# Hybrid pooling/SSD layer on one core: the scan's tables in one stretch, rounded sums, a weight split behind the mixer's last square, first loads on two queues, clearing later

## The chip, the cores and the metric

One Trainium2 chip, one core. The time is device microseconds of a whole execution of the kernel, the median of three executions. One execution of the kernel before was also taken by the profiler; views of that profile and its trace are what is read below. Engines are called by their names in the profile: PE is TensorE (its matmuls; PEld its weight loads), DVE VectorE, ACT ScalarE, POOL GpSimd, SP SyncE, which here issues most DMAs. "SPq" and "ACTq" rows are the DMA issues of those engines.

## The reference

One layer of a streaming encoder, for 256 frames of a new stream and 32 next frames of a running one. Both share all weights, so the kernel treats them as 288 columns. D_MODEL is 2048, the scan has 32 heads of 64 with a state of 128, and the feed-forward width is 5632. Cut to its core:

```python
xn   = rmsnorm(x, norm_mix_pre)
proj = xn @ w_in                                  # [u 1024 | z 2048 | xBC 2560 | dt 32]
y_pool = pool_mixer(u, ...)                       # trailing means over 2, 4, 8, 16 frames, times w_pool
xbc = silu(causal_dwconv(xbc)); dt = softplus(dt_raw + dt_bias)
acum = cumsum(dt * -exp(a_log)) in chunks of 64
y = chunked scan of xs, dt, B, C, acum, D         # decays exp(acum_i - acum_j) and exp(acum_last - acum)
y_ssd = rmsnorm per group (y * silu(z))
x  = x + rmsnorm(concat[y_pool, y_ssd] @ w_out, norm_mix_post)
hn = rmsnorm(x, norm_ffn_pre)
x  = x + rmsnorm((silu(gate) * val of causal_dwconv(hn @ w_up)) @ w_down, norm_ffn_post)
```

The outputs are the new x of both streams and all their new histories and states.

## The kernel before, in words

**Layout and the three products.** Features lie on the 128 partitions and the 288 frames along the columns. Every weight product in float32 is made of three rounded ones (`mm3`, L140 to L143): weight and activation are each split into a high half (rounded to fp32r) and a low half (the rest, rounded), and high x high, high x low and low x high are added in PSUM. The high half of a weight is a copy on ACT (L135), the low half a subtraction on DVE (L136), both in `split_w` in pieces of 1024 columns (512 where the piece is that narrow). `project` (L145 to L173) runs a group of output tiles over the depth of the weight: it fetches a piece (`fetch_w`, L116, issued by SP), splits it and issues its matmuls. Its arguments `wait`, `hold` and `behind` put the splits or the matmuls behind named instructions.

**Order.** A scheduler places the instructions on each engine by priorities and by its own model of the time. What is written `pin(...)` (`keep_in_program_order`) keeps the order of the program on its engine; `issue_after` puts an instruction behind another; `high_priority` draws it forward. Each engine takes its list in order.

**Start.** The input's first tile and the first weights are loaded in chunks (`CHUNKS`, L44: six of one row of 128, then five of two), each 768 columns wide, that is, six output tiles: four of B and C and two of the pool's input. SP issues all of these loads one after the other, but for the first third of chunk 0, which ACT issues (`first_load`, L207; `input_load`, L201; order L215 to L227). Chunk 0 is loaded and split in three column pieces (`PIECES`, L205), chunk 1 is loaded whole and split in three pieces, later chunks in one (`prepare`, L269 to L308: the input's halves at L281 and L284, the weight's at L293 and L297; for chunk 0 the first high third is made by DVE at L304, the others by ACT at L302, the lows by DVE at L307). `BUSY` (L45) matmuls on a constant tile (L264) run ahead of the first real ones. In chunk 0 the 18 matmuls go by half first and column block second (L344). GpSimd clears eight padded buffers for the convolutions (`ebuf`, `ubuf`, L330 to L332); they are first needed behind the last chunk. Squares of the input (L314, L317) are added up along the way; their sum over the partitions is one float32 matmul with ones, `prs` (L348), in the middle of the last chunk but one, and gives the root-mean-square factor `rstd` (L351, L352). The 32 columns of dt follow in float32 (L361).

**Scan's tables.** While TensorE goes on with the x part of the input projection, dt, its running sums `g` (32 heads on partitions, 416 columns in three blocks) and the decays `dec` are made on DVE and ACT (L471 to L510). They are turned so that frames lie on partitions: for each of three blocks, three transposes of 32 x 128 (`g`, `dt`, `dec`) into a PSUM tile of its own (L517 to L519) and two copies out. Then `pwq` (L526: three small matmuls that copy the last 32 rows of the turned decays to three places), `phv` (L535, L536: per-head factors spread over partitions), and `pcb`, the products of B and C, once for each of two groups (L552 to L554), masked into `cbt` (L555 to L558). Each of these stands where the scheduler puts it between the weight matmuls. Behind them come eight quads of heads (`ssd_quad`, L585), whose DVE and ACT work builds decay matrices and whose 16 float32 matmuls `py` each (L616 to L622) stand between weight matmuls. `sel`, `pick` and `sel64` (L376 to L378) are small constant tables for `phv`.

**Sums of the gated groups.** `rstd_all` (L662) sums squares over partitions by one float32 matmul with ones and takes the root and its reciprocal: `rg0` (L752) and `rg1` (L774) for the two groups of the scan, `r2` (L1086) for the feed-forward.

**Mixer's end.** The last output tile of w_out goes through `mix_out` (L842). The sum of the squares of all tiles but the last, `msum`, is rounded on ACT (L863) and its low half made on DVE (L864); the last tile is squared on ACT (L860), rounded on DVE (L861), its low half made on DVE (L864). Four rounded matmuls add the four parts over partitions (`psum_m`, L869), among the matmuls of the scan's final state (L950, L951). Then the root on ACT (`rm`, L1002) and its reciprocal on DVE (L1003), and for each of 16 tiles the scaling, the residual and the split of `hn` (L1014 to L1024), on which the first matmuls of the up projection wait. That projection's first call (`up`, L1077; L1100) has four groups of weights: three of 256 columns and one of 128, each in depths of four, so the last group's piece is 512 wide. All pieces of its first depth may be split before `hn` is there; later depths are held behind the first `hn` (`hold`).

Of the kernel before, what the change touches and what calls it, by code (L numbers as in the profile page):

```python
# [44 lines left out]
BUSY = 14  # L45
# [11 lines left out]
def body(  # L57
# [87 lines left out]
    def project(view, groups, acts, ksplit, before=None, done=None, spare=(), hold=(), behind=None, wait=()):  # L145
# [7 lines left out]
        for i, (kb, n) in enumerate(ksplit):  # L153
# [5 lines left out]
            for raw, (c0, w) in zip(raws, groups):  # L159
                parts = split_w(raw, kb, n, w, tuple(wait) + ((after or ()) if m0 else ()) + (hold if i else ()))  # L160
# [40 lines left out]
    def input_load(k0, k1):  # L201
        c = slice(KD + NT * k0 if k0 else 0, KD + NT * k1)
        pin(sp.dma_start(out=xg[:, c], in_=x_g[:, c]))
# [3 lines left out]
    def first_load(i):  # L207

        kb, n = CHUNKS[i]
        raw = wpool.tile([P, n, NB], F32, tag="raw" if n > 1 else ("hi", "lo")[i % 2], name="raw")  # L210
        for j, c in enumerate((slice(0, NB),) if i else PIECES):
            pin((sp if i or j else act).dma_start(out=raw[:, :, c], in_=w_first[:, kb : kb + n, c]))
        raws.append(raw)
# [3 lines left out]
    for i, (k0, k1) in enumerate(zip(INPUT[:-1], INPUT[1:])):  # L217
        input_load(k0, k1)
# [50 lines left out]
    def prepare(i):  # L269
# [19 lines left out]
        if i:  # L289
            for t in tiles:  # L290
                high(t)
            for c in PIECES if i == 1 else (slice(0, NB),):
                pin(act.activation(hi[:, :, c], raw[:, :, c], AF.Copy))  # L293
            for t in tiles:
                low(t)
            for c in PIECES if i == 1 else (slice(0, NB),):
# [26 lines left out]
    for i, (kb, n) in enumerate(CHUNKS):  # L323
# [4 lines left out]
        if i == 5:  # L328
            first_load(10)
            with tc.issue_after(lows[-1].ins):  # L330
                for e in ebuf + ubuf:
                    pin(pool.memset(e, 0.0))  # L332
# [4 lines left out]
        if i == len(CHUNKS) - 2:  # L337
            pin(dve.tensor_tensor(sq2[:, :NT], sq2[:, :NT], sq2[:, NT:], op=ALU.add))
        w = ahead_w.pop(0)
# [3 lines left out]
        if i == 0:  # L343
            products.sort(key=lambda q: (q[0], q[3]))  # L344
        for q, (r, m, k, x) in enumerate(products):
            if i == len(CHUNKS) - 2 and q == 24:
                p_ = aux([P, NT], "prs")
                pin(pe.matmul(p_, ones, sq2[:, :NT], start=True, stop=True))  # L348
# [23 lines left out]
    sel = const.tile([HEADS, 2], F32, name="sel")  # L372
    pick = const.tile([HEADS, NX], F32, name="pick")
    sel64 = const.tile([HEADS, 2, 64], F32, name="sel64")
    with tc.issue_after(last_split[1].ins):
        dve.tensor_reduce(sel, id32.rearrange("h (t r) -> h r t", r=2), axis=AX.X, op=ALU.add)  # L376
        dve.tensor_reduce(pick, id32.rearrange("h (t r) -> h t r", r=2), axis=AX.X, op=ALU.add)
        dve.tensor_copy(sel64, sel.unsqueeze(2).broadcast_to([HEADS, 2, 64]))  # L378

# [4 lines left out]
    mp = mixer.enter_context(tc.tile_pool(name="mixer", bufs=1))  # L384
    sc_stage = const.tile([P, 2, 3, NXC], F32, name="sc_stage")
# [109 lines left out]
    g = mp.tile([HEADS, 4, MW], F32, tag="m", bufs=2, name="g")[:, 0, :]  # L495
# [11 lines left out]
    dec = htile("dec", tag="gsum")  # L507
    for (o, n), go, last in zip(BLK, (0, 256, 384), (255, 383, 415)):
        act.activation(dec[:, o : o + n], g[:, go : go + n], AF.Exp, bias=g[:, last : last + 1], scale=-1.0)
    dve.tensor_tensor(dec, dec, dt, op=ALU.mult)  # L510


    tok = mp.tile([P, 3, 2, HEADS], F32, name="tok")
    tokd = const.tile([P, 3, HEADS], F32, name="tokd")
    for b, (o, go) in enumerate(((0, 0), (P, 256), (TAIL, MW - P))):
        p_ = aux([P, 3, HEADS], "ptok")
        pe.transpose(p_[:, 0, :], g[:, go : go + P], id32)  # L517
        pe.transpose(p_[:, 1, :], dt[:, o : o + P], id32)
        pe.transpose(p_[:, 2, :], dec[:, o : o + P], id32)  # L519
        dve.tensor_copy(tok[:, b, :, :], p_[:, 0:2, :])  # L520
        dve.tensor_copy(tokd[:, b, :], p_[:, 2, :])

    p_ = aux([P, HEADS], "pwq")
    wq = const.tile([P, HEADS], F32, name="wq")
    for j in range(3):
        pe.matmul(p_[NS * j : NS * (j + 1), :], ident[:, P - NS :], tokd[:, 2, :], start=True, stop=True)  # L526
    dve.tensor_copy(wq[: 3 * NS], p_[: 3 * NS])
# [6 lines left out]
    p_ = aux([P, NX + HEADS], "phv")  # L534
    pe.matmul(p_[:, :NX], sel64.rearrange("h r q -> h (r q)"), hv[:, :NX], start=True, stop=True)  # L535
    pe.matmul(p_[:, NX:], ones[:HEADS, :], hv[:, NX:], start=True, stop=True)  # L536
# [12 lines left out]
    for gi in range(2):  # L549
        blocks_out(b_d, gi, bc[gi], mp, 2)  # L550
        p_ = aux([P, MW], "pcb")
        pe.matmul(p_[:, 0:256], bc[gi][:, 0:P], bc[2 + gi][:, 0:NP_], start=True, stop=True)  # L552
        pe.matmul(p_[:, 256:384], bc[gi][:, P:NP_], bc[2 + gi][:, P:NP_], start=True, stop=True)
        pe.matmul(p_[:, 384:], bc[gi][:, TAIL:], bc[2 + gi][:, NP_:], start=True, stop=True)  # L554
# [107 lines left out]
    def rstd_all(sq, scale, name, pin=False):  # L662

        p_ = aux([P, NT], "psum_t")
        ins = pe.matmul(p_, ones, sq, start=True, stop=True)
        if pin:
            tc.keep_in_program_order(ins)
            sums_at.append(ins)
        with tc.high_priority(offset=800 if pin else 0):
# [73 lines left out]
    for i in range(NX // 2):  # L743
# [7 lines left out]
        if i == 5:  # L751
            rg.append(rstd_all(gsum[0], 0.25 / 1024, "rg0"))  # L752
# [21 lines left out]
    rg.append(rstd_all(gsum[1], 0.25 / 1024, "rg1"))  # L774
# [62 lines left out]
    ones_r = op_.tile([P, P], F32R, name="ones_r")  # L837
    act.activation(ones_r, ones, AF.Copy)
# [3 lines left out]
    def mix_out(p_):  # L842
# [9 lines left out]
        else:  # L852
            with tc.high_priority(offset=400):
# [3 lines left out]
                for i, q in enumerate((msum, last_sq)):  # L857
                    h_ = op_.tile([P, NT], F32R, tag="sq", bufs=2, name="mhi")
                    if i:
                        pin(act.activation(q, p_, AF.Square))  # L860
# [3 lines left out]
                    pin(dve.tensor_tensor(parts[i], q, h_.bitcast(F32), op=ALU.subtract))  # L864
                    parts.append(h_)

# [500 lines left out]
```

## Time and profile before

| | |
|---|---|
| median of three executions | 1331.42 us (1331.05 to 1332.49) |
| the profiled execution | 1331.79 us |
| its span in the profile | 1330.1 us |
| instructions | 25269 |
| DMA traffic | 251.74 MB, mean 189 GB/s |
| input projection's start (first chunk to the dt columns) | 5.69 to 48.4 us of the span |
| scan's tables | about 100 to 117 us |
| mixer's end | 472 to 479 us |

The span runs from the first to the last recorded instruction; the execution's own time holds 1.7 us more. In the views, times are microseconds from the span's start. A row of the timeline gives start and busy time, engine, line and operation, what it writes and reads with the shapes, and, in brackets, how long the engine had been idle before it and what ended that. "x4" is a run of four such instructions shown as one row. The chain of waits follows the work that ended last back from the end: its rows give the start, the time that the piece adds and the engine, tile and line. The busy time of a matmul in the timeline overlaps with its neighbours'; the step from one start to the next is what it costs. A table by stretches gives each engine's busy share (instructions in brackets), the granted clock of TensorE, the busy share of the DMA engines and GB/s.

### The profile page before, as it was taken

To read this page: it belongs to the slowest core of one execution; us is meant where nothing else is said; L and a number is where in the kernel's file an instruction comes from. 1 tells how busy PE (TensorE), PEld (TensorE's weight loads), DVE (VectorE), ACT (ScalarE), POOL (GpSimd) and SP (SyncE) were. 2 spreads that over 40 slices of the span, in tenths; PEclk is the share of its full clock that TensorE was granted. 3 is DMA by queue.
4 is the path that set the end of the run, shared out by engine and by line. 5 is a ranking of instruction groups with operands and counts; after the bars stand their busy time and mean duration, and the time that the engine had idled before them with its cause. 6 is when DMAs were issued, how large, how long until landed. Compare 5 with 4: busy or idle time off the path is not lost.

```text
span 1330.1 us, 25269 instructions
## 1 busy us (share of the span) xinstructions
PE 1321.7 (99%) x10057; PEld 1309.2 (98%) x10057; DVE 894.9 (67%) x1512; ACT 672.3 (51%) x1007; POOL 242.4 (18%) x391
## 2 busy tenths in 40 slices
PE   9999999999999999999999999999999999999998
PEld 8999999999999999999999999999999999999997
DVE  7899987879555688976766743345666666654454
ACT  7557767446543466544444433334444444444442
POOL 2332321222232210211211200001111111201110
PEclk9999999999999999999999999999999999999999
DMA  8568875455576467766545445455544555466663
GB/s 336 186 209 266 274 237 174 160 185 203 205 223 203 155 182 243 194 181 193 170 162 162 157 166 169 153 178 169 180 159 159 171 171 166 159 227 187 208 176 113
DMA packets 108885, 251.74 MB, mean 189 GB/s; under 512 B 64608, under 2 KB 72704, under 8 KB 86240
## 3 DMA queue, kind: packets, MB, share of 16 engines
q1 hardware_dynamic: 103712, 234.68, 54.9%
q0 software_dynamic: 4672, 14.95, 3.5%
q8 instruction: 78, 1.28, 0.4%
q10 hardware_dynamic: 384, 0.52, 0.1%
q14 instruction: 39, 0.32, 0.1%
HBM read 237.11 MB, written 13.00 MB: 188 GB/s over the span
## 4 chain that ended last, share of the span: by engine, by line
PE 98%; DVE 1%; DMA 0%; ACT 0%; SPq 0%; issue 0%
PE acc L141 30%; PE acc L143 30%; PE acc L142 30%; PE acc L354 2%; PE acc_x L354 1%; PE py L616 1%; PE acc L1228 0%; DMA xg<-in_x_g 0%; PE acc L1229 0%; PE acc_t L1251 0%; PE acc_x L142 0%; PE acc_x L141 0%; PE acc_x L143 0%; PE py L618 0%; DVE wlo L136 0%
## 5 line engine op out<-in xcount | busy, mean ns | idle before, releaser
L136 DVE TENSOR_TENSOR wlo<-raw,whi 128x1024 fp32r<-128x1024 f32 (+1 forms) x396 | 472.6, 1195 | 321.0 <-ACT whi L135 319.4
L135 ACT ACTIVATE whi<-raw 128x1024 fp32r<-128x1024 f32 (+1 forms) x396 | 408.4, 1033 | 488.4 <-PE acc L142 404.5
L141 PE MATMUL acc<-hn,whi 128*128 128x288 f32 x1376 | 403.9, 295 | 0.4 <-ACT hn L1019 0.4
L142 PE MATMUL acc<-hn,whi 128*128 128x288 f32 x1376 | 403.6, 294 | 0.1
L143 PE MATMUL acc<-hn,wlo 128*128 128x288 f32 x1376 | 403.3, 294 | 0.0
L142 PEld LDWEIGHTS acc<-hn,whi 128*128 128x128 f32 x1376 | 259.7, 189 | 0.4 <-DVE hn L1020 0.3
L143 PEld LDWEIGHTS acc<-hn,wlo 128*128 128x128 f32 x1376 | 259.7, 189 | 0.0
L141 PEld LDWEIGHTS acc<-hn,whi 128*128 128x128 f32 x1376 | 257.1, 187 | 0.9 <-ACT hn L1019 0.8
L142 PE MATMUL acc<-fa,whi 128*128 128x288 f32 x660 | 195.4, 296 | 0.0
L141 PE MATMUL acc<-fa,whi 128*128 128x288 f32 x660 | 195.4, 296 | 0.0
L143 PE MATMUL acc<-fa,wlo 128*128 128x288 f32 x660 | 195.0, 295 | 0.0
L141 PE MATMUL acc<-xn,whi 128*128 128x288 f32 x608 | 180.9, 297 | 0.0
L143 PE MATMUL acc<-xn,wlo 128*128 128x288 f32 x608 | 178.9, 294 | 0.0
L142 PE MATMUL acc<-xn,whi 128*128 128x288 f32 x608 | 178.8, 294 | 0.0
L142 PEld LDWEIGHTS acc<-fa,whi 128*128 128x128 f32 x660 | 124.4, 188 | 0.0
L141 PEld LDWEIGHTS acc<-fa,whi 128*128 128x128 f32 x660 | 124.0, 188 | 0.0
L143 PEld LDWEIGHTS acc<-fa,wlo 128*128 128x128 f32 x660 | 123.8, 188 | 0.0
L1055 POOL COPY fc_stage<-ebuf 128x4 f32<-128x4 f32 x88 | 26.1, 296 | 502.5 <-DVE ebuf L1054 460.8
L142 PEld LDWEIGHTS acc<-xn,whi 128*128 128x128 f32 x608 | 114.9, 189 | 0.1
L143 PEld LDWEIGHTS acc<-xn,wlo 128*128 128x128 f32 x608 | 114.7, 189 | 0.1
L141 PEld LDWEIGHTS acc<-xn,whi 128*128 128x128 f32 x608 | 113.9, 187 | 0.9 <-issue 0.5
L1061 DVE SCALAR_TENSOR_TENSOR fc<-ebuf,cols,fc 128x290 f32<-128x290 f32 x176 | 90.5, 517 | 2.9 <-ACT fc L1059 0.3
(336 smaller groups left out, 1780.3 us busy)
## 6 DMA issues: line engine op xcount, KB each, us to landing
raw<-in_w_up SPq DMA_DIRECT2D x80, 1024.0 KB, 5.1
raw<-in_w_in SPq DMA_DIRECT2D x38, 1024.0 KB, 5.2
raw<-in_w_down SPq DMA_DIRECT2D x32, 1024.0 KB, 4.9
raw<-in_w_out SPq DMA_DIRECT2D x24, 1024.0 KB, 5.4
raw<-in_w_down SPq DMA_DIRECT2D x16, 768.0 KB, 4.4
raw<-in_w_up SPq DMA_DIRECT2D x14, 512.0 KB, 3.7
gb<-g_d POOLq DMA_DIRECT2D x8, 832.0 KB, 6.9
raw<-in_w_first SPq DMA_DIRECT2D x5, 768.0 KB, 11.7
```

What stands on the lines that cost most here:

```text
L135: act.activation(hi, raw[:, k : k + n, :], AF.Copy)
L136: dve.tensor_tensor(lo, raw[:, k : k + n, :], hi.bitcast(F32), op=ALU.subtract)
L141: then(pe.matmul(out, wh, a[:, 0, :], start=start, stop=False))
L142: then(pe.matmul(out, wh, a[:, 1, :], start=False, stop=False))
L143: then(pe.matmul(out, wl, a[:, 0, :], start=False, stop=stop))
L354: pin(pe.matmul(first[m], w[:, k, r * NB + m * P :][:, :P], xn[kb + k][:, x, :], start=kb + k + r + x == 0, stop=kb + k == KD - 1 and r == ...
L616: ins = pe.matmul(y[c, 0:256], xw[:, 0, f_], m[:, h, 0:256], start=True, stop=False)
L1055: pool.tensor_copy(fc_stage[:, :, :, i], e[:, 256:324].rearrange("p (s c) -> p s c", c=34)[:, :, 0:2])
L1061: dve.scalar_tensor_tensor(c, e[:, r_ : r_ + 290], f_w[:, r_, i : i + 1], c, op0=ALU.mult, op1=ALU.add)
```

## The change

It has seven edits.

1. First loads: the second third of chunk 0 and the second input load are issued by ACT, not by SP. Chunks 1 to 3 (before: chunk 1) are split in three pieces. Chunk 0's matmuls go first through the four column blocks of the first two pieces, high halves before low, and then through the two of the last piece. There are 12 filler matmuls, not 14.
2. Clearing: the eight buffers are cleared behind a small store of DVE into the first of them, in chunk 5's place in DVE's order, and no longer only placed behind the input's low half of chunk 6 (`issue_after`, which moves it in the scheduler's list; in the trace GpSimd runs these eight from 2.80 us on).
3. `prs`: the sum of squares is split by DVE into two halves, and two rounded matmuls with the constant tile take the place of the float32 one.
4. `rg0` and `rg1`: likewise, high half on ACT and low half on DVE, with a rounded tile of ones that is now made early and kept. `r2` stays float32.
5. Tables: `g`, `dt` and the decays lie under each other on 96 partitions of one tile. The decay is multiplied block by block; two copies bring dt's blocks to their place. Three transposes of 96 x 128 turn all three at once into one PSUM tile, which also takes `phv`. All these matmuls and both `pcb` products are pinned one behind the other. `pwq` is gone: DVE copies the 32 rows to the three places.
6. `sel`, `pick` and `sel64` move to the mixer's own memory, and their order in the program with it.
7. Mixer's end: the split of the up projection's last group (the 512-wide piece) at its first depth is put behind the last square on ACT and behind its low half on DVE.

The diff, cut:

```diff
-BUSY = 14
+BUSY = 12
...
-                parts = split_w(raw, kb, n, w, tuple(wait) + ((after or ()) if m0 else ()) + (hold if i else ()))
+                parts = split_w(raw, kb, n, w, tuple(wait) + ((after or ()) if m0 else ()) + (hold if i else tail if m0 + w // P == n_all else ()))
...
-            pin((sp if i or j else act).dma_start(out=raw[:, :, c], in_=w_first[:, kb : kb + n, c]))
+            pin((sp if i or j == 2 else act).dma_start(out=raw[:, :, c], in_=w_first[:, kb : kb + n, c]))
...
-        input_load(k0, k1)
+        input_load(k0, k1, sp if i else act)
...
-            for c in PIECES if i == 1 else (slice(0, NB),):
+            for c in PIECES if i < 4 else (slice(0, NB),):
...
-            with tc.issue_after(lows[-1].ins):
-                for e in ebuf + ubuf:
-                    pin(pool.memset(e, 0.0))
+            pin(dve.memset(ebuf[0][:, 0:1], 0.0))
+            for e in ebuf + ubuf:
+                pin(pool.memset(e, 0.0))
...
+            sq_r = xin.tile([P, 2 * NT], F32R, tag="sq", bufs=1, name="sq_r")
+            pin(dve.tensor_copy(sq_r[:, :NT], sq2[:, :NT]))
+            pin(dve.tensor_tensor(sq_r[:, NT:], sq2[:, :NT], sq_r[:, :NT].bitcast(F32), op=ALU.subtract))
...
-            products.sort(key=lambda q: (q[0], q[3]))
+            products.sort(key=lambda q: (q[1] < 2, q[0], q[3]))
...
-                pin(pe.matmul(p_, ones, sq2[:, :NT], start=True, stop=True))
+                for c in (slice(0, NT), slice(NT, 2 * NT)):
+                    pin(pe.matmul(p_, busy[:, 0:P], sq_r[:, c], start=c.start == 0, stop=c.start > 0))
...
-    g = mp.tile([HEADS, 4, MW], F32, tag="m", bufs=2, name="g")[:, 0, :]
+    turned = mp.tile([P, 4, MW], F32, tag="m", bufs=2, name="g")[: 3 * HEADS, 0, :]
+    g, dt_rows, dec_rows = (turned[HEADS * i : HEADS * (i + 1), :] for i in range(3))
...
-        act.activation(dec[:, o : o + n], g[:, go : go + n], AF.Exp, bias=g[:, last : last + 1], scale=-1.0)
-    dve.tensor_tensor(dec, dec, dt, op=ALU.mult)
+        act.activation(dec[:, go : go + n], g[:, go : go + n], AF.Exp, bias=g[:, last : last + 1], scale=-1.0)
+        dve.tensor_tensor(dec_rows[:, go : go + n], dec[:, go : go + n], dt[:, o : o + n], op=ALU.mult)
+    for o, n, go in ((0, P, 0), (P, NT - P, 256)):
+        dve.tensor_copy(dt_rows[:, go : go + n], dt[:, o : o + n])
+    small = []
+    def follow(ins):
+        return pin(ins) if small else small.append(ins)
...
-    for b, (o, go) in enumerate(((0, 0), (P, 256), (TAIL, MW - P))):
-        p_ = aux([P, 3, HEADS], "ptok")
-        pe.transpose(p_[:, 0, :], g[:, go : go + P], id32)
-        pe.transpose(p_[:, 1, :], dt[:, o : o + P], id32)
-        pe.transpose(p_[:, 2, :], dec[:, o : o + P], id32)
...
+    for b, go in enumerate((0, 256, MW - P)):
+        follow(pe.transpose(p_tok[:, b, :], turned[:, go : go + P], ident[: 3 * HEADS, : 3 * HEADS]))
...
+    for j in range(3):
+        dve.tensor_copy(wq[NS * j : NS * (j + 1)], p_tok[P - NS :, 2, 2 * HEADS :])
...
+        else:
+            act.activation(sq_r[0], sq, AF.Copy)
+            dve.tensor_tensor(sq_r[1], sq, sq_r[0].bitcast(F32), op=ALU.subtract)
+            for i in range(2):
+                pe.matmul(p_, ones_r, sq_r[i], start=i == 0, stop=i == 1)
...
-                        pin(act.activation(q, p_, AF.Square))
+                        last_ops.append(pin(act.activation(q, p_, AF.Square)))
...
+            last_ops.append(last_lo)
...
+            tail=tuple(last_ops) if spare else (),
```

66 lines of the change are left out of this document (33 added, 33 removed).

## The prediction

> **What bounds the kernel now.** I read the page's shares and its chain first, then TensorE's spacing in the chain, then the timeline where that spacing breaks.
>
> ```profile
> span 1330.1 us, 25269 instructions
> PE 1321.7 (99%) x10057; PEld 1309.2 (98%) x10057; DVE 894.9 (67%) x1512; ACT 672.3 (51%) x1007; POOL 242.4 (18%) x391
> PE 98%; DVE 1%; DMA 0%; ACT 0%; SPq 0%; issue 0%
> 14.66 1.60 PE acc L354 x12
> 39.45 0.48 PE prs L348 x2
> ```
>
> TensorE is busy 99% of the span and is 98% of the chain, so only two things count: TensorE work that goes away, and the few places where it stands. Rounded matmuls of 288 columns follow each other every 1.60/12 = 0.133 us. A plain float32 sum of the same width takes 0.48 us, as two instructions, and so costs 3.6 rounded ones. The other engines have room on average (67% and 51%); they matter only where a matmul waits for one of them.
>
> **The start.** From 12.25 us on TensorE has no gap until past 48; before that it has several.
>
> ```profile
> 1.29 3.65 PE L264 MATMUL acc_x<-busy 128*128 128x288 f32 x14 [1.29 <-DVE busy L191]
> 2.66 0.94 SPq L212 DMA_DIRECT2D raw<-in_w_first  x2
> 4.03 1.37 POOL L332 MEMSET ubuf<- 128x350 f32 x4
> 4.20 1.34 DVE L304 CAST w<-raw 128x256 fp32r<-128x256 f32 x1 [2.96 <-DMA raw<-in_w_first]
> 5.69 0.77 PE L354 MATMUL acc<-xn,w 128*128 128x288 f32 x4 [0.75 <-DVE w L304]
> 5.89 1.08 DVE L307 TENSOR_TENSOR w<-raw,w 128x256 fp32r<-128x256 f32 x3
> 8.13 1.03 ACT L293 ACTIVATE w<-raw 128x256 fp32r<-128x256 f32 x3 [1.58 <-DMA raw<-in_w_first]
> 8.60 2.04 PE L354 MATMUL acc<-xn,w 128*128 128x288 f32 x12 [0.29 <-ACT w L293]
> 9.94 0.54 ACT L281 ACTIVATE xn<-xg 128x288 fp32r<-128x288 f32 x1 [0.77 <-DMA xg<-in_x_g]
> 11.29 0.50 PE L354 MATMUL acc<-xn,w 128*128 128x288 f32 x2
> 12.25 1.60 PE L354 MATMUL acc<-xn,w 128*128 128x288 f32 x10 [0.46 <-DVE w L297]
> ...
> 473.37 0.30 DVE L861 CAST mhi<-last_sq 128x288 fp32r<-128x288 f32 x1
> ```
>
> The DMA engines in the stretches of a microsecond (the last two columns are their busy share and GB/s):
>
> ```profile
> 3.00:4.00 1.00, 1.00 (x6) 1.00 (x5) 0.00 (x0) 0.00 (x0) 1.00 (x4) 1.00 0.95 280
> 4.00:5.00 1.00, 0.95 (x5) 0.67 (x3) 0.80 (x1) 0.91 (x2) 1.00 (x4) 1.00 0.78 155
> ```
>
> The first cast takes 1.34 us and ends at 5.54, 0.14 us after GpSimd's clearing (4.03 + 1.37 = 5.40); a cast of 288 columns at the mixer's end takes 0.30. I read this as the cast standing behind the clearing. With the clearing later the first weights are ready at about 4.5, and the first matmul starts near 4.6 and not 5.69. Chunk 0 has 18 matmuls, 2.4 us; its lower halves come from VectorE from 4.5 + 0.50 on, 1.08 for all three, so by 6.1, and the two column blocks of the late piece now come last. It ends near 7.1.
>
> Chunk 1 starts 0.47 us behind the landing of its weights (8.13 to 8.60) and takes until 11.29, 2.69 us. That load was SP's fifth issue and is now its third; two issues of 0.47 us (0.94 for a pair) make it 0.94 us earlier, and in 4.00:5.00 the DMA engines had room (0.78). So chunk 1 runs about 7.7 to 10.35. Chunk 2 waits for inputs that landed at 9.94, now about 9.0: 0.54 for the input, then two pieces of its weights (0.34 each, a third of 1.03) bring the first third at 10.2, its lower half (0.36, a third of the three at 1.08) at 10.6, in time for its third matmul; the wait of 0.46 us at 12.25 is gone. Chunk 2 starts gapless at 10.35; before, 12.25 less the 0.27 of its two done matmuls is 11.98. The gain is 1.6, and I take **1.5**. If no landing moves, chunk 1 stays at 8.60, chunk 2 follows at 11.29 thanks to the pieces, and 0.7 is left. The upper end is 1.9: two queues moved 280 GB/s in 3.00:4.00 where one moved 155 a microsecond later. ACT's two more issues lie where it waits for its first data, as the cast does at 4.20. The clearing now stands behind a store of VectorE in chunk 5, near 18 to 21, beside VectorE work with two float32 sources, of which no row here shows one beside the clearing: if these were held like the cast, about 1 us (1.34 - 0.30) of the gain would go.
>
> [...]
>
> **The sums.** prs becomes two rounded matmuls: 0.48 - 0.27 = 0.21 saved. VectorE copies and subtracts first (0.30 + 0.46): its last addition, below, ended at 37.28, so 38.1, and TensorE would arrive at 39.45 - 1.5 = 37.95.
>
> ```profile
> 36.82 0.46 DVE L338 TENSOR_TENSOR sq<-sq 128x288 f32<-128x288 f32 x1
> ```
>
> VectorE's own stream starts earlier too, by what the landings gain; I take **0.2**, bounds -0.4 to 0.21. rg0 and rg1, the same product over 288 columns, save 0.21 each, **0.4**: the new ACT and VectorE steps stand several us ahead of the sums in their queues. If they were late it would cost what they take, 0.9 each.
>
> **The scan's tables.** Four interruptions become one, at the same matmul count as between the second and the third.
>
> ```profile
> 100.31 0.29 PE L143 MATMUL acc<-xn,wlo 128*128 128x288 f32 x1
> 101.83 0.29 PE L141 MATMUL acc<-xn,whi 128*128 128x288 f32 x1
> ...
> 107.24 0.29 PE L143 MATMUL acc<-xn,wlo 128*128 128x288 f32 x1
> 107.47 0.37 PE L519 MATMUL ptok<-ident,dec 32*128 32x32 f32 x3
> 108.00 0.29 PE L142 MATMUL acc<-xn,whi 128*128 128x288 f32 x1
> ...
> 111.31 0.29 PE L143 MATMUL acc<-xn,wlo 128*128 128x288 f32 x1
> 111.72 0.39 PE L535 MATMUL phv<-hv,sel 32*128 32x16 f32 x2
> 112.28 0.70 PE L552 MATMUL pcb<-bc 128*128 128x256 f32 x2
> 113.39 0.30 PE L142 MATMUL acc<-xn,whi 128*128 128x288 f32 x1
> ...
> 115.54 0.59 PE L552 MATMUL pcb<-bc 128*128 128x256 f32 x2
> 116.34 0.38 PE L143 MATMUL acc<-xn,wlo 128*128 128x288 f32 x1
> 116.56 0.29 PE L141 MATMUL acc<-xn,whi 128*128 128x288 f32 x1
> ```
>
> Start to start, less 0.13 for each ordinary matmul in it: 101.83 - 100.31 with four, 1.00; 108.00 - 107.24 with two, 0.50; 113.39 - 111.31 with two, 1.82; 116.56 - 115.54 with one, 0.89: together 4.2. The one stretch keeps phv (112.28 - 111.72 = 0.56), the two products (0.80 to 0.90 each) and one entry and one exit (about 0.1 each). pwq goes, and three transposes of 96 rows take the place of nine of 32; before, three took 0.30 (107.47 to 107.77), so 0.3 to 0.6. That is 2.8, a gain of **1.4**, 0.9 to 1.7.
>
> It adds a wait: all transposes now stand behind the last decay product.
>
> ```profile
> 102.97 0.44 DVE L510 TENSOR_TENSOR dec<-dec,dt 32x288 f32<-32x288 f32 x1
> 104.58 1.23 DVE L136 TENSOR_TENSOR wlo<-raw,whi 128x1024 fp32r<-128x1024 f32 x1 [0.74 <-ACT whi L135]
> ```
>
> The product ended at 103.41, plus some 0.6 us of new copies ahead of it; the stretch starts at about 107.4 (both less the start's gain): 3.4 us of reserve. Behind it on VectorE stand the copies of the tables and work of quads 0 and 1, about 8 us between two weight halves. The half of 104.58 ends at 105.81 and is first read at 116.34, so halves lie over 10 us ahead here, and I cost it at nothing; past that cover every microsecond is one of the kernel's. Quad 0's matmuls move 50 matmuls back, quad 1's 46; the third keeps its place.
>
> **The mixer's end.** TensorE waits for a chain that begins with the last square.
>
> ```profile
> 471.93 0.14 PE acc L142
> ...
> 472.09 0.64 ACT whi L135
> 472.76 0.69 DVE wlo L136
> 473.71 0.47 DVE mlo L864
> 474.22 0.41 PE psum_m L869
> ...
> 478.75 0.67 PE acc L141 x3
> ```
>
> A 512-wide split stood ahead of the square on ACT (until 472.73) and ahead of its rounding on VectorE (until 473.45). Moved behind, the square can start when its sum is out, about 472.2 (the last matmul of the sum leaves the chain at 472.07); it takes some 0.4, the rounding 0.30 and the low half 0.47, so the chain is at 473.4 where it was at 474.18. The last sum then comes at 473.6 (TensorE has other matmuls ahead of it), not 474.22, and all after it is **0.65** earlier: up to 0.72, and 0 if the split is late for its own matmuls. It fits: ACT has 0.64 for it between the square and the root behind the last sum, VectorE 0.69 before the reciprocal of that root. What is late next is the same chain: hn's first matmul still waits.
>
> **Sum.** 1.5 + 0.2 + 0.4 + 1.4 + 0.65 = 4.15, call it 4.2. The profiled execution took 1331.79 (span 1330.1 and 1.7 around it), so 1327.6; the median of the runs is 0.37 below that execution: **1327.2**.
>
> **Rivals.**
> - *The landings don't move.* The loads are fluent anyway (0.95 share in 3.00:4.00) and chunk 1 stays at 8.60. The start gives 0.7: the run would take 1328.0. Against it: 0.78 at 4.00:5.00.
> - *The clock opens late.* The fillers run at 3.65/14, 0.26 each, the chunks at 0.133, though the granted clock is 1.00 in both stretches: the full rate came with the fillers' end. Twelve end near 4.4. If the opening slips by as much as the fillers lasted, 3.4 us, chunk 0 takes 18 x 0.26 = 4.7 and ends at 9.3 for 7.1, chunk 1 starts up to 1.6 late: 1329.0. For it: the filler is shorter. Against: real work follows at once. [...]
> - *Slower: the one stretch stands.* TensorE takes its queue in order, so a late decay product stops all weights' matmuls behind it, one for one. It decides from 3.4 us of lateness; from 7.6 the whole gain is gone, from 10.3 the kernel is over 0.2% slower, 1334.1. For it: the product's last exponential stands on ACT behind a split that had to wait for TensorE (104.58 shows VectorE waiting for such a split). Against: that wait was 0.74.
> - *The change doesn't do what it says on the sums and tables.* New waits of the splits, in the worst 0.9 a sum, eat the stretch's 1.4 and the sums' 0.6: 1329.2; with unmoved landings 1330, no difference. For it: three splits are added to VectorE, which is 67% busy. Against: none is near its use.
>
> **Chances.** Forecast 0.63, landings 0.14, clock 0.07, sums and small stalls 0.11, slower stretch 0.05. 0.2% is 2.7 us, about what a measurement of this kernel can tell from no change; faster than 1331.42 less that, 1328.76, are the forecast, the landings and the lightest of the stalls: 0.78; the other stalls and the clock are within it: 0.17; slower: 0.05. All terms at their upper ends (1.9, 0.2, 0.4, 1.7, 0.72) give 1331.4 - 4.9 = 1326.5, less 0.4 for the runs' own spread 1326.1; 1329.3 takes in landings, clock and the stalls up to 2.1.
>
> **What would show it.** The first real matmul near 4.6; the gapless stretch from 10.3 to 10.5; one interruption of about 2.8 near 105.8 and none by transposes elsewhere; sums at 0.27; hn's first matmul 0.65 earlier relative to the state matmuls' start. I am wrong if TensorE gets waits beside VectorE between 110 and 135, if the cast is still long, or if chunk 1 still starts after 8.

## The result, and the profile after

| | before | changed |
|---|---|---|
| median | 1331.90 us (1330.84 to 1332.54, 21 executions) | 1329.66 us (1328.80 to 1331.38, 21 executions) |
| ratio to before | | 0.9984, 95% interval 0.9978 to 0.9990 |
| profiled execution, span | 1331.79, 1330.1 us | 1331.38, 1329.7 us |

The kernel is 2.2 us faster, where 4.2 had been forecast, and 1329.66 lies above the range. The profiled execution is one of the two longest of the 21, which will matter below.

The page of the changed kernel: the shares look as before, 14 recorded matmuls fewer.

```profile
span 1329.7 us, 25260 instructions
PE 1320.6 (99%) x10043; PEld 1309.7 (98%) x10043; DVE 897.3 (67%) x1523; ACT 673.2 (51%) x1013; POOL 247.4 (19%) x391
```

The start in its timeline:

```profile
4.02 0.30 DVE L304 CAST w<-raw 128x256 fp32r<-128x256 f32 x1 [2.78 <-DMA raw<-in_w_first]
4.46 2.89 PE L358 MATMUL acc<-xn,w 128*128 128x288 f32 x12
6.90 0.54 ACT L281 ACTIVATE xn<-xg 128x288 fp32r<-128x288 f32 x1 [1.48 <-DMA xg<-in_x_g]
7.34 1.02 ACT L293 ACTIVATE w<-raw 128x256 fp32r<-128x256 f32 x3
7.98 2.00 PE L358 MATMUL acc<-xn,w 128*128 128x288 f32 x12
...
37.82 0.43 PE L352 MATMUL prs<-sq_r,busy 128*128 128x288 f32 x2
```

The cast takes 0.30 us where it took 1.34, the first real matmul starts at 4.46 where it started at 5.69, and the first sum begins 1.47 us earlier (its first matmul at 37.82; before, at 39.29):

```profile
39.29 0.65 PE L348 MATMUL prs<-sq,ones 128*128 128x288 f32 x2
```

The scan's tables, one interruption of TensorE from 106.15 to the second ordinary matmul behind it:

```profile
106.15 0.41 PE L530 MATMUL ptok<-ident,g 96*128 96x96 f32 x3
107.05 0.70 PE L560 MATMUL pcb<-bc 128*128 128x256 f32 x2
107.95 0.68 PE L560 MATMUL pcb<-bc 128*128 128x256 f32 x2
108.83 0.38 PE L143 MATMUL acc<-xn,wlo 128*128 128x288 f32 x1
109.04 0.29 PE L141 MATMUL acc<-xn,whi 128*128 128x288 f32 x1
```

109.04 - 106.15 less one ordinary matmul is 2.76 us: the forecast's 2.8. The mixer's end in the timeline:

```profile
471.91 0.39 PE L965 MATMUL pst<-xh,bt_h 128*128 128x512 f32 x1
472.11 0.41 ACT L873 ACTIVATE last_sq<-acc 128x288 f32<-128x288 f32 x1
473.46 0.35 PE L884 MATMUL psum_m<-mlo,ones_r 128*128 128x288 f32 x1
477.36 0.53 ACT L1035 ACTIVATE hn<-mg,cols 128x288 fp32r<-128x288 f32 x1 [0.56 <-DVE mg L1031]
```

and the same two ends in the kernel before:

```profile
472.03 0.39 PE L950 MATMUL pst<-xh,bt_h 128*128 128x512 f32 x1
478.16 0.54 ACT L1019 ACTIVATE hn<-mg,cols 128x288 fp32r<-128x288 f32 x1 [0.54 <-DVE mg L1015]
```

From the first state matmul to hn's copy it is 477.36 - 471.91 = 5.45 us, before 478.16 - 472.03 = 6.13: 0.68 less. So every term came in this execution, and their sum should show. Nearly all of it is taken back at one place, quad 0. The timeline there, rows of VectorE, GpSimd's queue, ACT and TensorE:

```profile
119.55 0.56 POOL L590 DMA_DIRECT2D xk<-xs_d  x1
125.62 0.96 DVE L603 TENSOR_TENSOR xk<-xk,tok 128x768 f32<-128x768 f32 x1 [5.55 <-DMA xk<-xs_d]
126.50 1.89 DVE L612 TENSOR_TENSOR m<-m,cbt 128x1664 f32<-128x1664 f32 x1
...
119.30 1.58 ACT L611 ACTIVATE m<-m 128x1664 f32<-128x1664 f32 x1
...
126.13 0.30 PE L142 MATMUL acc<-xn,whi 128*128 128x288 f32 x1
128.44 0.65 PE L624 MATMUL py<-m,xk 128*64 128x256 f32 x4 [2.01 <-DVE m L612]
129.34 1.08 PE L624 MATMUL py<-m,xk 128*64 128x256 f32 x4
131.15 0.61 PE L143 MATMUL acc<-xn,wlo 128*128 128x288 f32 x1
...
132.92 0.29 PE L141 MATMUL acc<-xn,whi 128*128 128x288 f32 x1
```

Read it from below. TensorE stands for 2.01 us because quad 0's mask product (L612) is late. Its input was ready at 119.30 + 1.58 = 120.88, but ahead of it in VectorE's list stands L603, the scaling of quad **2**'s tokens, and that one waits 5.55 us for a transfer that GpSimd issued at 119.55. In the kernel before, the order was the other way, and quad 0's matmuls lay between 122.64 and 124.98 (timeline of before):

```profile
118.58 1.88 DVE L604 TENSOR_TENSOR m<-m,cbt 128x1664 f32<-128x1664 f32 x1
...
130.42 0.95 DVE L595 TENSOR_TENSOR xk<-xk,tok 128x768 f32<-128x768 f32 x1
...
122.64 0.29 PE L142 MATMUL acc<-xn,whi 128*128 128x288 f32 x1
...
124.98 0.30 PE L141 MATMUL acc<-xn,whi 128*128 128x288 f32 x1
```

In this execution the wait has a second price. Stretches of a microsecond of the changed kernel; the column behind POOL is the granted clock:

```profile
128.00:129.00 1.00, 0.56 (x6) 0.42 (x8) 1.00 (x2) 0.00 (x0) 0.00 (x0) 1.00 0.00 0
129.00:130.00 1.00, 1.00 (x18) 0.82 (x16) 1.00 (x4) 0.00 (x0) 0.00 (x0) 0.69 0.00 0
130.00:131.00 1.00, 1.00 (x14) 0.82 (x12) 1.00 (x3) 0.63 (x1) 0.55 (x1) 0.50 0.00 0
131.00:132.00 1.00, 1.00 (x8) 0.94 (x6) 1.00 (x3) 0.95 (x4) 0.57 (x1) 0.50 0.03 8
132.00:133.00 1.00, 1.00 (x7) 1.00 (x6) 1.00 (x4) 1.00 (x5) 0.19 (x1) 0.60 0.56 90
```

The clock is granted at half for about 3.4 us (the missing shares add up to 0.31 + 0.50 + 0.50 + 0.40 = 1.7 us of full rate), so quad 0 and the matmuls behind it cost about 1.6 us more. In sum quad 0 costs 126.13 to 132.92, less eight ordinary matmuls, 5.7 us, where each quad costs 2.1 in the kernel before (124.98 - 122.64 less two). So 5.7 - 2.1 = 3.6 us of what the terms brought are lost here in this execution, and its span is only 0.4 shorter.

The lower clock is not the usual case. For the executions without a profile the record has the mean granted clock alone, and it is 1.000 in 13 of the 21, the median one among them. A loss of 1.7 us would have left 0.9987, so in these 13 the clock did not fall like this.

### The profile page after: what moved, and what is told of

It reads as the page before. It is cut to its first block, busy times and chain, and to the rows that moved or that the text cites. A ratio compares the mean times of both kernels' runs of the same rounds, so it can differ in the third digit from the quotient of the medians.

```text
span 1329.7 us, 25260 instructions
## 1 busy us (share of the span) xinstructions
PE 1320.6 (99%) x10043; PEld 1309.7 (98%) x10043; DVE 897.3 (67%) x1523; ACT 673.2 (51%) x1013; POOL 247.4 (19%) x391
## 4 chain that ended last, share of the span: by engine, by line
PE 98%; DVE 1%; ACT 0%; issue 0%; ACTq 0%; DVEq 0%
PE acc L141 30%; PE acc L143 30%; PE acc L142 30%; PE acc L358 2%; PE acc_x L358 1%; PE py L624 1%; PE acc L1245 0%; PE acc L1246 0%; PE acc_x L142 0%; PE acc_x L141 0%; PE acc_x L143 0%; PE py L626 0%; PE acc_x L264 0%; PE acc_t L1268 0%; DVE wlo L136 0%
## 5 line engine op out<-in xcount | busy, mean ns | idle before, releaser
L1066 POOL COPY ebuf<-cols 128x2 f32<-128x2 f32 x88 | 74.2, 844 | 110.4 <-DVE fc L1077 52.3
```

The costliest lines, as they stand in the source:

```text
L1066: pool.tensor_copy(e[:, 258:260], hist_f[:, :, i])
```

## The experiments

Theory: **held mask** (all terms came, quad 0's mask stands on VectorE behind a product that waits for quad 2's tokens). Rivals: the one stretch displaced the quads so that other inputs are late too; the wait comes from the earlier start or another edit; the terms are worth less in executions without the profiler. Each kernel was timed in five rounds beside the kernel before. The kernel before came out at medians of 1331.89 to 1332.18 in these sets of rounds, so a difference of 0.3 us between kernels of different sets means nothing.

**order_quads.**

```diff
+            if q == 2:
+                order.enter_context(tc.issue_after(m_ops[q - 2].ins))
             dve.tensor_tensor(o, o, w, op=ALU.mult)
```

> The changed kernel with one placement altered: the scaling of quad 2's tokens (xk) goes behind the masking of quad 0's decays (m) in VectorE's list; nothing is left out. Theory 'held mask': every term of the forecast came, and then TensorE lost 2.0 us waiting for quad 0's mask, which stood on VectorE behind a product that waited for quad 2's tokens, and about 1.6 us more because its granted clock was halved after that wait. Then this kernel is about 4.2 us under the kernel before (1327.2 to 1328), with no wait of TensorE over 0.3 us at quad 0 and the granted clock at 1.00 from 120 to 140. Rival 'displaced quads': the one stretch moved quad 0 into a place where other inputs are late too (exponentials, weight halves), so another wait takes the place: under 1 us faster than the changed kernel.

1328.25 us, ratio 0.9973 (0.9964 to 0.9983), 3.65 under the kernel before, where about 4.2 had been expected; its profile has a span of 1326.0, 4.1 under. VectorE and TensorE in its timeline:

```profile
121.37 1.89 DVE L616 TENSOR_TENSOR m<-m,cbt 128x1664 f32<-128x1664 f32 x1 [0.83 <-ACT m L615]
125.16 0.96 DVE L607 TENSOR_TENSOR xk<-xk,tok 128x768 f32<-128x768 f32 x1 [1.90 <-DMA xk<-xs_d]
...
126.31 0.30 PE L142 MATMUL acc<-xn,whi 128*128 128x288 f32 x1
126.54 0.65 PE L628 MATMUL py<-m,xk 128*64 128x256 f32 x4
127.44 0.63 PE L628 MATMUL py<-m,xk 128*64 128x256 f32 x4
128.66 0.29 PE L141 MATMUL acc<-xn,whi 128*128 128x288 f32 x1
```

(`m_ops` holds the mask products.) The two rows changed places in VectorE's list (the scheduler also moved rows around them, and quad 1 stands four matmuls later), and the wait and the low clock are gone. Quad 0 stands behind as many weight matmuls as in the changed kernel, so "displaced quads" falls. Against the changed kernel's median it is 1.4 us, not 3.6: the profiled execution lost more than the median one. A clock that did not fall is one reason; how much the transfer's landing differs in executions without a profile is not on record.

**no_tables.** The changed kernel with the tables of before (nine transposes, `pwq`, `phv` in a tile of its own, no `follow`).

```diff
-    for b, go in enumerate((0, 256, MW - P)):
-        follow(pe.transpose(p_tok[:, b, :], turned[:, go : go + P], ident[: 3 * HEADS, : 3 * HEADS]))
+    for b, (o, go) in enumerate(((0, 0), (P, 256), (TAIL, MW - P))):
+        p_ = aux([P, 3, HEADS], "ptok")
+        pe.transpose(p_[:, 0, :], g[:, go : go + P], id32)
...
```

> The changed kernel with the scan's tables as before (nine transposes, pwq, nothing pinned); nothing is left out. 'Held mask': the inverted order came with the tables, so it is gone; start 1.5, sums 0.6 and mixer's end 0.65 stay: 2.75 us under the kernel before, about 1329.0, clock at 1.00 around quad 0. Rival 'the other parts are worth less without the profiler': 1 us or less under the kernel before.

1329.66 us, ratio 0.9985 (0.9976 to 0.9994), 2.24 under before: no wait at quad 0, and against order_quads the tables are worth 1.4 us, as forecast. In the changed kernel they were worth nothing: 1329.66 with and without them. The rival that the terms are worth less without the profiler had expected 1 us or less. But 2.75 had been expected by the theory: half a microsecond is missing here as in order_quads, so that part of the loss does not come from the tables.

**tables_only.** The other way round: the kernel before with this edit alone.

```diff
-    g = mp.tile([HEADS, 4, MW], F32, tag="m", bufs=2, name="g")[:, 0, :]
+    turned = mp.tile([P, 4, MW], F32, tag="m", bufs=2, name="g")[: 3 * HEADS, 0, :]
...
```

> The kernel before with the tables' edit alone; nothing is left out. 'Held mask': VectorE's list shows quad 2's scaling ahead of quad 0's mask here too, so the 1.4 us of the tables are taken back by 2.0 to 3.6 us of wait and low clock: 0.5 to 2.2 us slower than the kernel before. Rival 'the wait comes from the earlier start or from the other edits': 1.4 us faster than the kernel before, no wait at quad 0.

1331.75 us, ratio 1.0004 (0.9996 to 1.0013), from 1330.75 to 1334.93: the widest spread of all. VectorE and TensorE in its timeline:

```profile
127.82 0.96 DVE L598 TENSOR_TENSOR xk<-xk,tok 128x768 f32<-128x768 f32 x1 [5.29 <-DMA xk<-xs_d]
128.70 1.89 DVE L607 TENSOR_TENSOR m<-m,cbt 128x1664 f32<-128x1664 f32 x1
...
130.64 0.65 PE L619 MATMUL py<-m,xk 128*64 128x256 f32 x4 [2.38 <-DVE m L607]
```

The same wait without any other edit, so it belongs to the tables' edit: that rival falls too. The size expected was missed (no difference instead of 0.5 to 2.2 slower). In its profile the clock stays at 1.00 behind a wait of 2.38 us, where it fell to 0.50 for about 3.4 us behind one of 2.01 in the changed kernel. Why one wait cost clock and a longer one did not, two executions do not show.

**order_no_last_split.**

```diff
-            tail=tuple(last_ops) if spare else (),
```

> As order_quads, but the up projection's 512-wide split is free to stand ahead of the mixer's last square, as in the kernel before; nothing is left out. If the mixer's end is worth what the profile shows, 0.65 to 0.7 us slower than order_quads; if the wait behind it only moves to another place, the same.

1328.95 us, ratio 0.9979 (0.9970 to 0.9988): 0.70 above order_quads. The mixer's end is worth its 0.65.

**start_undone.** order_quads with the whole start of before.

```diff
-BUSY = 12
+BUSY = 14
...
-            pin((sp if i or j == 2 else act).dma_start(out=raw[:, :, c], in_=w_first[:, kb : kb + n, c]))
+            pin((sp if i or j else act).dma_start(out=raw[:, :, c], in_=w_first[:, kb : kb + n, c]))
...
-            pin(dve.memset(ebuf[0][:, 0:1], 0.0))
+            with tc.issue_after(lows[-1].ins):
...
```

> As order_quads, with the whole start as in the kernel before: one queue but for the first piece, early clearing, 14 fillers, chunks 2 and 3 whole, chunk 0's matmuls by half first; nothing is left out. If the start is worth the 1.5 us that the profile showed, 1.5 us slower than order_quads (about 1329.8); if the order of DMA landings, which differs between the profiles of one start by up to 0.8 us, eats part of it, 0.7 to 1.2.

1329.83 us, ratio 0.9986 (0.9978 to 0.9995): 1.6 above order_quads, as expected. In its profile, though, 0.9 us is no part of the start: from the start of the last matmul to the end of the span, in which the last outputs land, it takes 5.68 us, where it takes 5.67 in float_sums and 4.79 to 4.81 in all other profiles. Whether its other executions end like this is not on record. The four kernels that follow take this start apart.

**clear_early.** Only the clearing as before.

```diff
-            pin(dve.memset(ebuf[0][:, 0:1], 0.0))
-            for e in ebuf + ubuf:
-                pin(pool.memset(e, 0.0))
+            with tc.issue_after(lows[-1].ins):
+                for e in ebuf + ubuf:
+                    pin(pool.memset(e, 0.0))
```

> As order_quads, but GpSimd clears the buffers as in the kernel before, from about 2.8 us on; nothing is left out. 'The cast stands behind the clearing': VectorE's first cast takes some 1.3 us again and ends 0.14 us behind the clearing, the first real matmul starts near 5.6, chunk 0 ends about 8.1 and chunk 1 follows at once: 0.3 to 0.5 us slower than order_quads. Rival 'the cast was slow for another reason (its weights' pieces)': it takes 0.30 with the clearing beside it, no difference.

1329.50 us, ratio 0.9983 (0.9974 to 0.9992): 1.25 above order_quads, more than expected. Its timeline:

```profile
4.02 1.36 POOL L332 MEMSET ubuf<- 128x350 f32 x4
4.06 1.48 DVE L304 CAST w<-raw 128x256 fp32r<-128x256 f32 x1 [2.82 <-DMA raw<-in_w_first]
5.68 1.04 PE L358 MATMUL acc<-xn,w 128*128 128x288 f32 x6 [1.14 <-ACT w L302]
```

The cast stands behind the clearing: 1.48 us beside it, 0.29 to 0.30 in the kernels without it. That this costs 1.25 us and not 0.3 to 0.5 was not explained by its profile, which is the shortest of its executions (1327.63): its real matmuls step by 0.13 us from 5.89 on. In the profiles of tables_only and start_undone, where the first one comes as late (5.67 and 5.68), they step by 0.24 until 9.6 and 10.4. I take it that most executions of clear_early step like those, but did not show it.

**one_queue.**

```diff
-            pin((sp if i or j == 2 else act).dma_start(out=raw[:, :, c], in_=w_first[:, kb : kb + n, c]))
+            pin((sp if i or j else act).dma_start(out=raw[:, :, c], in_=w_first[:, kb : kb + n, c]))
...
-        input_load(k0, k1, sp if i else act)
+        input_load(k0, k1)
```

> As order_quads, but SP issues the second third of chunk 0 and the second input load again; ACT issues only the first third; nothing is left out. 'Issue time sets the landings': chunk 1's weights land 0.8 to 0.9 us later and TensorE, which goes through chunks 0 and 1 without a gap in order_quads, waits for them: 0.5 to 0.8 us slower than order_quads. Rival 'the landings follow the DMA engines' load': the same landings, no difference.

1328.52 us, ratio 0.9976 (0.9966 to 0.9986): 0.27 above order_quads, less than can be told apart; 0.5 to 0.8 had been expected. In its profile chunk 1's weights landed later (their copy starts at 7.87, for 7.34 to 7.38), but with the same order of issues it starts at 7.03 in tables_only and 7.22 in start_undone, so this does not show that the order made them late. The second input landed earlier (its copy at 6.32, for 6.90 to 6.94).

**more_fillers.**

```diff
-BUSY = 12
+BUSY = 14
```

> As order_quads, but with 14 filler matmuls and not 12; nothing is left out. In the profiles so far the first real matmuls step by 0.24 us until a moment between 5.4 and 9.6 and by 0.13 after it, at a granted clock of 1.00 in all of them, and that moment differs between executions of kernels with the same start. 'Free-running opening': two more fillers only move the first real matmul to about 4.9, and chunk 1 still starts near 8: no difference beyond 0.3. Rival 'the fillers open it': a chunk 0 at the full rate, chunk 1 near 7.5 behind its landing, 0.3 to 0.5 us faster than order_quads and a narrower spread.

1328.40 us, ratio 0.9976 (0.9967 to 0.9985): no difference from order_quads, as the first of the two expectations had it.

**whole_chunks.**

```diff
-            for c in PIECES if i < 4 else (slice(0, NB),):
+            for c in PIECES if i == 1 else (slice(0, NB),):
```

> As order_quads, but chunks 2 and 3 are split whole and not in three pieces; nothing is left out. By the prediction the pieces took away the wait of 0.46 to 0.7 us in chunk 2: TensorE waits there again, 0.4 to 0.7 us slower. If chunk 2's inputs now land early enough, no difference.

1327.99 us, ratio 0.9974 (0.9964 to 0.9983): no difference, where 0.4 to 0.7 slower had been expected. The pieces, to which the prediction gave the gapless chunk 2, bring nothing that can be told apart.

**float_sums, prs_float, groups_float.** Sums as float32 matmuls again: all three, the first alone, the two groups' alone.

```diff
-                pe.matmul(p_, ones_r, sq_r[i], start=i == 0, stop=i == 1)
+            pe.matmul(p_, ones, sq, start=True, stop=True)
...
```

> As order_quads, but the three sums of squares are float32 matmuls again; nothing is left out. Three times 0.21: 0.6 us slower than order_quads, each sum 0.48 and not 0.27 in the chain; if the added splits cost something elsewhere, less than that.

> As order_quads, but the first sum of squares (prs) is a float32 matmul again, the sums of the two groups stay rounded; nothing is left out. float_sums took 1.4 us more where 0.6 was expected. If the first sum is worth its 0.21: 0 to 0.3 us slower than order_quads, and the rest of the 1.4 belongs to the groups' sums. If the excess came with the first sum or its splits, 0.8 to 1.1 us slower.

> As order_quads, but the sums of the two groups are float32 matmuls again, the first sum (prs) stays rounded; nothing is left out. If the sums are worth their 0.21 each: 0.4 to 0.6 us slower than order_quads. float_sums stood 1.4 us above order_quads and prs_float 0.3: if the excess of 0.8 comes with the groups' sums, 1.0 to 1.2 us slower.

1329.68 (0.9986, 0.9977 to 0.9995), 1328.51 (0.9975, 0.9965 to 0.9984) and 1329.07 us (0.9980, 0.9971 to 0.9988): 1.4, 0.3 and 0.8 above order_quads. The parts add up to 1.1; 0.6 was expected. (Compared with the kernel before of its own rounds, groups_float is 0.6 above order_quads and not 0.8.) The chains show each float32 sum at 0.48 and each rounded pair of the groups at 0.26 to 0.27. The first sum's pair is 0.27 only where its split is ready. In four profiles TensorE waits for it between the two matmuls or ahead of them, and the sum costs 0.47 (order_quads), 0.62 (order_quads_again), 0.67 (more_fillers) and 0.83 (input_on_sp): there nothing is saved. In order_quads:

```profile
37.84 0.63 PE L352 MATMUL prs<-sq_r,busy 128*128 128x288 f32 x2
```

So it stays open why float_sums loses more than 0.6. Its profile has the longer end of 5.67 us, 0.9 more than order_quads, which is no part of the sums.

**order_quads_again.** The same kernel once more.

> The same kernel as order_quads, for its own interval beside the three others: 3.65 us under the kernel before, within 0.3. Its start in the profile shows how far the second input's landing moves between two executions of one kernel: if the landings are drawn anew in each execution, it differs from 6.94 us by some tenths; if they are fixed by the program, it is within 0.1.

1328.24 us, ratio 0.9974 (0.9964 to 0.9984), and a span of 1327.3 in its profile where order_quads had 1326.0. The copy of the second input in order_quads and, in the second fence, in order_quads_again:

```profile
6.94 0.54 ACT L281 ACTIVATE xn<-xg 128x288 fp32r<-128x288 f32 x1 [1.59 <-DMA xg<-in_x_g]
```

```profile
7.86 0.53 ACT L281 ACTIVATE xn<-xg 128x288 fp32r<-128x288 f32 x1 [2.54 <-DMA xg<-in_x_g]
8.76 1.52 PE L358 MATMUL acc<-xn,w 128*128 128x288 f32 x7 [0.80 <-ACT w L293]
```

Landings differ from execution to execution: 0.9 us between two of one kernel, and with 7.86 chunk 1 starts at 8.76, no earlier than in the kernel before.

**input_on_sp.**

```diff
-        input_load(k0, k1, sp if i else act)
+        input_load(k0, k1)
```

> As order_quads, but the second input load is SP's again (behind the third piece of chunk 0, as in the kernel before); ACT keeps the second third of chunk 0; nothing is left out. In the profiles the second input landed at 6.90 to 7.86 us where ACT issued it and at 5.99 to 6.32 where SP did. If ACT's issue is the reason, it lands near 6.2 here, chunk 1 starts at 7.6 to 7.9 in every execution, and the kernel is 0.2 to 0.5 us faster than order_quads. If what it competes with is the reason (chunk 0's second third, issued earlier), it lands near 7 here too, and nothing changes.

1327.94 us, ratio 0.9970 (0.9958 to 0.9983), the lowest median of all; from order_quads it cannot be told apart. The input is copied at 5.28 here. SP issued its load at 1.72 us, ACT in order_quads at 1.74, so not the moment of the issue but the engine that issues goes with the late landing. But two waits appear in its timeline, the second behind quad 0:

```profile
37.59 0.90 PE L352 MATMUL prs<-sq_r,busy 128*128 128x288 f32 x2
37.57 0.46 DVE L341 TENSOR_TENSOR sq_r<-sq,sq_r 128x288 fp32r<-128x288 f32 x1
...
127.02 0.96 DVE L607 TENSOR_TENSOR xk<-xk,tok 128x768 f32<-128x768 f32 x1 [2.90 <-DMA xk<-xs_d]
127.89 1.22 DVE L136 TENSOR_TENSOR wlo<-raw,whi 128x1024 fp32r<-128x1024 f32 x1
129.16 0.40 PE L143 MATMUL acc<-xn,wlo 128*128 128x288 f32 x1 [0.64 <-DVE wlo L136]
```

TensorE waits longer than in order_quads for the first sum's new split (the sum costs 0.83), and the tokens of quad 2, landed at 127.0, still hold the low half of a weight behind them.

**tokens_later.**

```diff
-                order.enter_context(tc.issue_after(m_ops[q - 2].ins))
+                order.enter_context(tc.issue_after(m_ops[q - 1].ins))
```

> As input_on_sp, but quad 2's token scaling stands behind quad 1's mask, so that two low halves of weights stand ahead of it on VectorE; nothing is left out. In the profile of input_on_sp the tokens landed at 127.0, the low half behind their scaling ended late and TensorE waited 0.64 us for it behind quad 0. If VectorE's list behind the tokens is what is left of the loss, that wait is gone, quads 0 and 1 cost 2.08 each, and the kernel is 0.2 to 0.5 us faster than input_on_sp (1327.4 to 1327.7). If the low half is late for another reason (its high half), no difference.

1328.51 us, ratio 0.9974 (0.9965 to 0.9983), from 1327.42 to 1330.25: not faster. In its profile, the shortest span of all (1325.7), the wait of 0.64 is gone and both quads cost 2.1. What lengthens its other executions is open; its list has the next such pair, quad 3's tokens ahead of quad 2's mask, and VectorE waited there 2.39 us for the transfer without holding TensorE this time.

## Why the prediction was wrong, step by step

- *The start, 1.5.* Right in size: 1.47 in the profile, 1.6 against start_undone. The cast stood behind the clearing, as read. But the size came in part by luck, for its parts were others than forecast: by the medians the clearing alone is 1.25 of it, and the earlier loads and the pieces, to which the prediction gave most of it, are worth 0.27 and nothing, neither to be told from zero. Chunk 1's weights were copied 0.8 earlier than in the kernel before (7.34 for 8.13), but landings of 7.03 and 7.22 with the old order do not let this count as shown. The second input, issued by ACT, was copied 0.9 later (6.90 for 6.02), and TensorE waits 0.2 to 0.8 us at chunk 1 in seven of the eleven profiles in which ACT issued it. So 1.47 is the best case: in the eight profiles with the whole new start the first sum begins between 37.82 and 38.76. The runs show beside this that a load can land later when ACT issues it, at the same moment: the second input was copied at 6.90 where ACT issued it at 1.74 (changed kernel), at 5.28 and 5.98 where SP issued it at 1.72 (input_on_sp, tokens_later).
- *The landings don't move.* This rival came in part, as just told.
- *The late clock.* This rival came true in part and cost little in this profile: the first seven real matmuls of the changed kernel step by 0.24 to 0.40 us until 6.53, but chunk 1's input and weights, copied from 6.90 and 7.34 on, would have kept TensorE waiting anyway. Its working was off in small things: the fillers step by 0.24 us and not 0.26, fourteen of them last 3.65 and not 3.4 (that the opening slips by 3.4 was an estimate; the steps here became short 2.1 us behind the first real matmul, 4.46 to 6.53), and 1327.2 + 1.6 is 1328.8 and not 1329.0.
- *The sums, 0.6.* The groups' sums cost 0.26 to 0.27 for 0.48, as forecast. The first sum does so in this profile too, but in four others it waits for its split, which the prediction had as its lower bound. By the medians the three are worth more (1.1 to 1.4), and the reason is open.
- *The tables, 1.4.* One interruption of 2.76 for the forecast's 2.8, and 1.4 between no_tables and order_quads. The wait for the last decay product did not come: it ended at 102.83 in the timeline, 3.3 us ahead of the stretch.
- *The step that failed*: "Behind it on VectorE stand the copies of the tables and work of quads 0 and 1 ... I cost it at nothing", and the sentence after it, "Quad 0's matmuls move 50 matmuls back, quad 1's 46; the third keeps its place." The cover that I named was the lead of the weight halves, and they were not late. But the quads' own work has no such lead, and the second sentence holds the trap: where quad 0 moves back and quad 2 stays, quad 2's token scaling comes to stand ahead of quad 0's mask in VectorE's list, which is worked off in order: VectorE stood 5.55 us ahead of the scaling, though the mask's input was ready at 120.88. (That the moving back is why the scheduler changed the order is my reading; shown is that the order comes with the tables' edit.) The scheduler fixes VectorE's order before the kernel runs, so it could have been compared. I asked only what stands between two weight halves, not which row waits for a transfer. In place of nothing it cost 2.0 us of wait and 1.6 of clock in the profile, 1.4 in the median. The prediction's own sign of being wrong, a wait beside VectorE between 110 and 135, came at 128.44.
- *The mixer's end, 0.65.* Right: 0.68 in the profile, 0.70 in order_no_last_split.
- *New waits of the splits.* This rival came at the first sum alone, and smaller than its 0.9: at most 0.6 (0.83 for 0.27, in input_on_sp).
- *The slower rival* named a standing TensorE behind the tables, but at the wrong place: a late product ahead of the stretch, not a late mask 20 us behind it.
- *The sum.* order_quads and order_quads_again show what the forecast described: 3.65 and 3.76 under before, for 4.15. So of the 1.9 us that the changed kernel misses, 1.4 are the held mask, and 0.4 to 0.5 are missing without it. Waits of that size stand in single profiles: at chunk 1, at the first sum, behind quad 2's tokens, and one that is in no term, at a place that no edit touches. At the very end TensorE waits for `diag`, which ACT makes, 0.67 us in the kernel before and 1.00 in the changed kernel; in the two profiles of order_quads' kernel it is 0.76 and 1.07. How much of the 0.4 to 0.5 in the median belongs to each was not measured.

## What to carry to other kernels

When an edit moves a group of instructions, compare the order on every engine for pairs that changed places, and ask of each which row waits for a transfer: on VectorE, whose list is worked off in order, an early row of a later group held a late row of an earlier one (5.55 us for quad 2's transfer, and TensorE stood 2.01 for quad 0's mask). TensorE can pay twice for standing, the wait and the lower clock behind it (2.0 and 1.6 us in the changed kernel), though here only one of the two profiled waits did. Terms that are each right do not sum when one of them shifts work onto a transfer: 3.6 us of them were lost there in the profiled execution, 1.4 in the median.

## What the runs showed of the hardware

- After a wait of 2.01 us in the changed kernel TensorE's granted clock was 0.50 for about 3.4 us, starting some 0.9 us after work had begun again; after a wait of 2.38 us in tables_only it stayed at 1.00.
- The first matmuls step by 0.24 us and later ones by 0.13, at a granted clock of 1.00 in the records of both. In the profiles of the kernels with the new start, clear_early apart, the step changes between 5.3 and 7.3 us. With the old start it is 0.13 from 5.90 on in the kernel before, and changes at 9.6 and 10.4 in tables_only and start_undone.
- The second input load was copied at 6.18 to 7.86 us in the eleven profiles where ACT issued it, and at 5.28 to 6.32 in the six where SP did, issued at 1.73 to 1.74 and at 1.72 to 2.19.
- The first cast of 256 columns took 1.34 to 1.62 us beside GpSimd's clearing (four profiles) and 0.29 to 0.30 without it (thirteen).
